# Filler matmuls in planned gaps everywhere, not only in the normalisation zones

## The chip, the core and the metric

The kernel runs on one core of a Trainium2 chip. The metric is device time in microseconds from launch to end, the median of three runs. TensorE (PE) does matmuls and writes PSUM, VectorE (DVE) and ScalarE (ACT) work on PSUM and SBUF, GpSimd (POOL) on SBUF alone, and SyncE (SP) issues the DMAs. TensorE's clock has two levels in the records, 1.2 and 2.4 GHz; a granted clock of 0.50 is the lower one.

## The reference, cut to what matters

Two trunk layers run over 128 context tokens and 512 latent tokens that share every weight, in float32.

```
for l in range(DEPTH):                       # DEPTH = 2, D_MODEL = 1024
    shift1, scale1, gate1, shift2, scale2, gate2 = SiLU(cond) W_mod + b_mod
    u = LN(x) * (1 + scale1) + shift1
    x = LN_1(alpha * x + gate1 * W_out concat_heads[mLSTM | gated DeltaNet | retention | RWKV-7](u W_in))
    u = LN(x) * (1 + scale2) + shift2
    x = LN_2(alpha * x + gate2 * relu(u W_1)^2 W_2)
```

Each mixer has four heads of width 64 and scans forwards and backwards over chunks. DeltaNet and RWKV-7 need, for each 128 tokens, the inverse of a triangular matrix. The fillers of this case compute nothing that the reference asks for: their results are never read.

## The kernel before

**How the work is staged.** A layer has three parts. *Mixing*: weights of `w_in` come in as tiles `wr`, are split into a high part `wh` (ScalarE, sometimes VectorE) and a low part `wl` (GpSimd or VectorE), and are multiplied with the features `uh`, `ul` in three matmuls per block of 128 into PSUM tiles `pj` (`pgj` for the gates). Beside these dense projections run the scans: many small float32 matmuls whose results go through VectorE and ScalarE and back. `solve_blocks` and `inverse` (tiles `ei`, `ew`, `lv`) make the inverses, `step` walks the chunks (`pxx`, `pwx`, `pzz`), and at the end of a mixer stand its outputs (`poo`, `pqs`), its head norm on VectorE (`osum`), its transposes (`pt`), and the result `y`, which goes through DRAM and comes back as `yk`, `yh`, `yl`. *Output and normalisation*: `w_out` (tiles `pwo`), layer norms, transposes to features (`put`). *Feed-forward*: `pj` with features `vh`, `vl`, then `pff`. Modulation (`pmod`, `pmt`, `pmg`, `msb`) for layer 0 begins at once and goes on inside the mixing; that of layer 1 runs beside layer 0's feed-forward part. Of the eight blocks of `y`, the one made last is that of the second DeltaNet pair, and 195 of a layer's 240 `pwo` matmuls come behind its transposes.

**What sets the order.** Nothing is issued as it is written. `Plan.record` notes each operation as a node with an estimated duration. `Plan.schedule` (line 416) then plays the program forward on five engines with those estimates: whenever an engine is free it takes the ready node of highest priority for which PSUM and SBUF have room. `Plan.emit` (line 775 in every profile row) issues the nodes in the order of their planned starts, and each engine keeps strictly to this order. The planner also books how much matmul work TensorE has done lately (`recent - part`, in columns weighted by the cost of the type) and doubles the durations where it thinks the clock is low.

**Fillers.** Where TensorE's queue is empty in the plan, or holds only nodes that may wait a little longer (`early`), the planner may put in a filler: a float32 matmul of 128 x 128 constants (line 810, tile `warm`), which is two passes in the profile. It takes one of eight PSUM banks, must leave two free (`FB`), and isn't used in the first 12 planned microseconds (`FT0`). Before the change it must also be in a zone: a stretch of nodes marked by hand around `w_out`, the layer norms and the transposes to features (`thin()`, and `plan.zones.append` at line 2362). `floor` is the oldest node that has not been planned yet, and is what a zone is compared with. In a zone a filler goes in while the booked work is under 1.3 x 3100 (`FT`).

Of the kernel before, what the change touches and what calls it, by code (L numbers as in the profile page):

```python
# [213 lines left out]
class Plan:  # L214
# [201 lines left out]
    def schedule(self):  # L416
# [34 lines left out]
        caps, load, blocked, order = {}, {}, {}, {}  # L451
# [33 lines left out]
        FT, FT0, FB, FN = 1.3, 12.0, 2, 128  # L485
# [7 lines left out]
        now = 0.0  # L493
        done = 0
        floor = 0
# [3 lines left out]
        early = []  # L499
# [11 lines left out]
        hist, recent = collections.deque(), 0.0  # L511
# [20 lines left out]
        def pe_queue():  # L532
            tops = [(q[0], (128, 128), q) for q in (heaps["PE"],) if q]
            tops += [(q[0], m_, q) for m_, q in tiled.items() if q]
            best = min(tops, key=lambda x: x[0][:2], default=None)
            if dense and (best is None or dense[0][:2] < best[0][:2] or not warm or thin):
                best = (dense[0], (128, 128), dense)
            if best is None:
                while early and early[0][2].end is not None:
                    heapq.heappop(early)  # L540
                return early or None
            if best[1] != mode:
                same = [x for x in tops + ([(dense[0], (128, 128), dense)] if dense else []) if x[1] == mode]
                if same:
                    c = min(same, key=lambda x: x[0][:2])
                    if c[0][0] - best[0][0] < HY:
                        best = c
            return best[2]
# [11 lines left out]
        def filler(now):  # L560
            x = self.warm_tile().tile
            caps[x.key] -= 1
            x.seq = x.at = x.end_seq = floor
            load[x.key][floor] += 1
            x.alloc = True
            nd = Node()
            nd.eng, nd.nm, nd.idx, nd.tiles, nd.preds, nd.succs, nd.grp = "PE", "matmul", len(N) + len(out), [x], [], [], None
            nd.a, nd.k, nd.fn = (x.view()[:, 0:FN],) + self.warm(FN), {}, self.warm_fn
            nd.mem, nd.act, nd.mode = [("matmul", nd.fn, nd.a, nd.k)], self.activity("matmul", nd.a[0], nd.a), self.pe_mode(nd.a)
            nd.dur = self.pe_time(nd.mem)  # L570
            return nd, x

        def eligible(nd, t):
            must = nd.idx == floor
            used, take = {}, []
            for x in nd.tiles:
                if x.alloc:
                    continue
                if not must and x.kind == "psum" and nd.grp is None and not x.open and caps[x.key] - used.get(x.key, 0) <= RES:
                    return x.key, None  # L580
                if not room(x, used):
                    return x.key, None
                used[x.key] = used.get(x.key, 0) + 1
                take.append(x)
            if not must:
                for x in list(take):
                    for p in x.gate.values():
                        if p.end is None or p.end > t + 0.3:
                            return ("g", p), None
                    for p in x.late.values():  # L590
                        if p.end is None:
                            return ("g", p), None
                    for y in x.along:
                        if not y.alloc and y not in take:
                            if not room(y, used):
                                return y.key, None
                            used[y.key] = used.get(y.key, 0) + 1
                            take.append(y)
            return None, take
        gateb = {}  # L600
        wait = {}
        while True:
            progress = True
            while progress:
                progress = False
                for e in engs:
# [3 lines left out]
                    if e == "PE":  # L610
# [3 lines left out]
                        part = 0.0  # L614
                        if hist and hist[0][0] < now + LK - TICK:
                            a_, b_, c_ = hist[0]
                            part = c_ * (now + LK - TICK - a_) / (b_ - a_)
                        thin = recent - part < HM * 3100
                        warm = cols.get(k - 1, 0.0) >= 3100
                    while h or e == "PE" or soon[e]:  # L620
                        q = pe_queue() if e == "PE" else h or soon[e]
                        if e == "PE" and (q is None or q is early) and now > FT0 and recent - part < FT * 3100 and any(a <= floor < b for a, b in self.zones) and caps[self.bank] > FB:
                            nd, x = filler(now)
                            d = nd.dur + (SW if nd.mode != mode else 0.0)
                            mode = nd.mode
                            d *= 1 if warm else 2
                            hist.append((now, now + d, nd.act))
                            recent += nd.act
                            k = int(now / TICK + 1e-9)
                            cols[k] = cols.get(k, 0.0) + nd.act  # L630
                            nd.start = now
                            nd.end = free[e] = now + d
                            out.append(nd)
                            self.nfill += 1
                            heapq.heappush(ev, (free[e], cnt, 1, None)); cnt += 1
                            heapq.heappush(ev, (free[e] + 0.1, cnt, 2, x)); cnt += 1
                            progress = True
                            break
# [19 lines left out]
                        b, take = eligible(nd, now)  # L658
# [81 lines left out]
            now = max(now, ev[0][0])  # L740
# [1775 lines left out]
```

## Time and profile before

| | |
|---|---|
| runs | 2372.74, 2365.53, 2366.48 us |
| median | 2366.48 us |
| profiled execution, its own time | 2367.83 us |
| its span, first to last instruction | 2366.1 us |
| TensorE matmuls busy | 2149.7 us, 91% |
| VectorE / ScalarE / GpSimd busy | 66% / 40% / 33% |
| mean granted clock of TensorE | 0.953 |
| fillers in the program | 188 (376 passes) |

A profile row of the timeline has the start, the time from the start of the first to the end of the last of a merged group, engine, line, operation, output and inputs, shapes and count; in brackets is how long the engine sat idle before and who released it. The parts of the span, by the timeline: start to 56 us, mixing of layer 0 to about 643, output and normalisation to about 764, feed-forward to about 1246, and then the same for layer 1, whose mixing ends at about 1803.

### The profile page before, as it was taken

What the parts mean: (1) busy time and instruction counts of PE and PEld (TensorE: products, weight loads), DVE (VectorE), ACT (ScalarE), POOL (GpSimd) and SP (SyncE); (2) the same over time, 40 slices, a digit from 0 to 9 for tenths busy, and PEclk for the clock granted to TensorE, in tenths of its full rate; (3) what the DMA queues carried; (4) which work ended last, traced back from release to release, by engine and by line L of the source; (5) the groups of instructions that cost most, each with busy time, mean ns of one, the idle gap of its engine ahead of it and who ended that gap; (6) DMA issues with size and microseconds to landing.
All of it is one profiled execution on the core that took longest, in us unless ns stands there. A gap on an engine that the chain in (4) does not pass through costs nothing. (4 is left out here: it accounts for less than half of the span.)

```text
span 2366.1 us, 42824 instructions
## 1 busy us (share of the span) xinstructions
PE 2149.7 (91%) x16886; PEld 1887.9 (80%) x16886; DVE 1557.5 (66%) x3258; ACT 948.1 (40%) x2014; POOL 771.4 (33%) x687
## 2 busy tenths in 40 slices
PE   5998989988887999999979989899888799999997
PEld 2887778777677898889867878798777689999996
DVE  5576768686779657666687768679785843333357
ACT  3434244342335545445344443443441443333332
POOL 2141414433347333334353424324452710000023
PEclk7999989999798999999998989899899999999999
DMA  8132352626443444444541322313353412222242
GB/s 266 28 69 77 102 112 75 172 76 167 147 133 116 140 132 134 134 125 132 173 125 36 74 36 60 88 53 83 102 164 108 151 63 73 80 72 81 71 161 89
DMA packets 317453, 253.17 MB, mean 107 GB/s; under 512 B 91100, under 2 KB 240828, under 8 KB 317252
## 3 DMA queue, kind: packets, MB, share of 16 engines
q1 hardware_dynamic: 317252, 250.43, 37.1%
q8 instruction: 133, 2.18, 0.4%
q14 instruction: 68, 0.56, 0.1%
HBM read 226.14 MB, written 24.24 MB: 106 GB/s over the span
## 5 line engine op out<-in xcount | busy, mean ns | idle before, releaser
L775 ACT CAST wh<-wr 128x1024 fp32r<-128x1024 f32 x233 | 244.3, 1049 | 502.2 <-PE pff L775 214.1
L775 PE MATMUL pff<-wh,hid 128*128 128x512 f32 x1280 | 397.6, 392 | 0.2 <-ACT wh L775 0.2
L775 POOL TENSOR_TENSOR wl<-wr,wh 128x1024 fp32r<-128x1024 f32 x92 | 227.9, 2480 | 407.2 <-ACT wh L775 394.2
L775 DVE TENSOR_TENSOR wl<-wr,wh 128x1024 fp32r<-128x1024 f32 x142 | 186.5, 1313 | 208.8 <-ACT wh L775 208.7
L775 PE MATMUL pj<-uh,wl 128*128 128x256 f32 (+1 forms) x1056 | 312.6, 336 | 8.5 <-POOL wl L775 6.3
L775 PE MATMUL pj<-uh,wh 128*128 128x256 f32 (+1 forms) x1056 | 311.3, 336 | 9.6 <-ACT wh L775 6.3
L775 PE MATMUL pj<-ul,wh 128*128 128x256 f32 (+1 forms) x1056 | 311.9, 334 | 0.0
L775 PE MATMUL pj<-vh,wl 128*128 128x384 f32 (+1 forms) x1024 | 286.7, 312 | 3.5 <-POOL wl L775 3.2
L775 PE MATMUL pj<-vh,wh 128*128 128x384 f32 (+1 forms) x1024 | 284.4, 313 | 5.0 <-ACT wh L775 5.0
L775 PE MATMUL pj<-vl,wh 128*128 128x384 f32 (+1 forms) x1024 | 283.3, 312 | 0.0
L775 PEld LDWEIGHTS pff<-wh,hid 128*128 128x128 f32 x1280 | 238.8, 189 | 51.1 <-ACT wh L775 0.5
L775 PE MATMUL pff<-wl,hid 128*128 128x512 f32 x640 | 245.2, 396 | 9.3 <-POOL wl L775 8.7
L775 PEld LDWEIGHTS pj<-uh,wh 128*128 128x128 f32 x1056 | 194.9, 196 | 27.3 <-issue 10.5
L775 PEld LDWEIGHTS pj<-uh,wl 128*128 128x128 f32 x1056 | 194.9, 196 | 25.9 <-issue 9.9
L775 PEld LDWEIGHTS pj<-ul,wh 128*128 128x128 f32 x1056 | 195.8, 196 | 12.6 <-issue 8.3
L775 PEld LDWEIGHTS pj<-vh,wh 128*128 128x128 f32 x1024 | 186.9, 191 | 9.4 <-ACT wh L775 5.7
L775 PEld LDWEIGHTS pj<-vh,wl 128*128 128x128 f32 x1024 | 185.7, 191 | 6.5 <-POOL wl L775 3.8
L775 PEld LDWEIGHTS pj<-vl,wh 128*128 128x128 f32 x1024 | 185.9, 190 | 2.5 <-issue 1.4
L775 POOL TENSOR_TENSOR mac<-mac,mtm 128x512 f32<-128x512 f32 x77 | 112.4, 1460 | 183.9 <-ACT mtm L775 160.1
L775 DVE TENSOR_TENSOR hid<-sqr,hid 128x384 fp32r<-128x384 f32 (+1 forms) x126 | 77.5, 618 | 129.4 <-ACT hid L775 128.9
L775 DVE SCALAR_TENSOR_TENSOR mac<-wr,cc,mac 128x512 f32<-128x512 f32 x84 | 100.8, 1200 | 78.2 <-DMA wr<-in_w_mod 56.8
L775 POOL TENSOR_TENSOR acc<-acc,bc 128x512 f32<-128x512 f32 x16 | 27.3, 1729 | 382.6 <-DMA xr<-x1d 357.5
(502 smaller groups left out, 4249.5 us busy)
## 6 DMA issues: line engine op xcount, KB each, us to landing
wr<-in_w_ff SPq DMA_DIRECT2D x136, 512.0 KB
wr<-in_w_mod SPq DMA_DIRECT2D x96, 512.0 KB
wr<-in_w_in SPq DMA_DIRECT2D x66, 512.0 KB
wr<-in_w_out SPq DMA_DIRECT2D x32, 512.0 KB
dq<-rscr SPq DMA_DIRECT2D x20, 256.0 KB
dec<-rscr SPq DMA_DIRECT2D x16, 320.0 KB
x1d<-x SPq DMA_DIRECT2D x20, 256.0 KB
xr<-x1d SPq DMA_DIRECT2D x20, 256.0 KB
```

Source lines behind the costliest of these rows:

```text
L775: fn(*[res(v) for v in a], **{k_: res(v) for k_, v in k.items()})
```

## The change

One condition of the planner is widened. Outside the zones a filler may now go in too, if the work booked is under 3100 (without the factor 1.3). All other conditions stay. Nothing else in the kernel is edited.

```diff
--- before.py
+++ after.py
@@ -619,7 +619,7 @@
                     while h or e == "PE" or soon[e]:
                         q = pe_queue() if e == "PE" else h or soon[e]
-                        if e == "PE" and (q is None or q is early) and now > FT0 and recent - part < FT * 3100 and any(a <= floor < b for a, b in self.zones) and caps[self.bank] > FB:
+                        if e == "PE" and (q is None or q is early) and now > FT0 and recent - part < FT * 3100 and (any(a <= floor < b for a, b in self.zones) or recent - part < 3100) and caps[self.bank] > FB:
                             nd, x = filler(now)
```

Since the plan is made forward, a filler changes what is planned behind it, on all engines. The program before has 188 fillers, the program after 225. Numbers behind a name count tiles and differ between the two programs for the same tile.

The first place is TensorE at the start, where the first modulation tiles (`pmod`, with `pmt` and `pmg` behind each) meet the first transposes to features (`put`, whose inputs `xn` are normalised tokens). Before:

```order
L775 MATMUL pmg_253<-cst,msb_216 128x128
L775 MATMUL pmt_270<-msb_263,cst 32x128 x4
L775 MATMUL pmg_288<-cst,msb_263 128x128
L775 MATMUL put_299<-cst,xn_161 128x128
L775 MATMUL put_301<-cst,xn_161 128x128
L775 MATMUL put_303<-cst,xn_161 128x128
L775 MATMUL put_309<-cst,xn_161 128x128
L775 MATMUL put_313<-cst,xn_205 128x128
L775 MATMUL put_319<-cst,xn_205 128x128
L775 MATMUL put_327<-cst,xn_205 128x128
L775 MATMUL put_313<-cst,xn_243 128x128
L775 MATMUL pmod_336<-wr_165,cc 32x512 x2
```

and after:

```order
L775 MATMUL pmg_261<-cst,msb_218 128x128
L810 MATMUL warm_266<-cst 128x128
L810 MATMUL warm_270<-cst 128x128
L775 MATMUL pmt_285<-msb_268,cst 32x128 x4
L810 MATMUL warm_297<-cst 128x128
L810 MATMUL warm_304<-cst 128x128
L775 MATMUL pmg_309<-cst,msb_268 128x128
L810 MATMUL warm_311<-cst 128x128
L775 MATMUL put_314<-cst,xn_161 128x128
L775 MATMUL put_316<-cst,xn_161 128x128
L775 MATMUL pmod_320<-wr_165,cc 32x512 x2
```

Five fillers came in (a sixth stands further up), and six of the eight transposes moved behind the eight `pmod` rows that follow here. A `put` tile of `xn_161` is complete with one transpose; `put_313` needs the two that are seen.

The second place is TensorE in layer 0's mixing, at the `pmt` of a gate's modulation, whose bias comes by DMA; `pj_6547` and `pj_6554` (in the second list `pj_6556` and `pj_6558`) are the two halves of a projection. Before:

```order
L775 MATMUL pj_6291<-uh_478,wl_6262 128x256
L775 MATMUL pmt_6531<-msb_6451,cst 32x128 x4
L775 MATMUL pj_6547<-uh_317,wh_6517 128x384
L775 MATMUL pj_6554<-uh_317,wh_6517 128x256
L775 MATMUL pj_6547<-ul_325,wh_6517 128x384
L775 MATMUL pj_6554<-ul_325,wh_6517 128x256
L775 MATMUL pj_6547<-uh_317,wl_6536 128x384
```

and after:

```order
L775 MATMUL pj_6291<-uh_471,wl_6267 128x256
L810 MATMUL warm_6536<-cst 128x128
L810 MATMUL warm_6542<-cst 128x128
L775 MATMUL pmt_6544<-msb_6452,cst 32x128 x4
L810 MATMUL warm_6549<-cst 128x128
L810 MATMUL warm_6552<-cst 128x128
L775 MATMUL pj_6556<-uh_327,wh_6523 128x384
L775 MATMUL pj_6558<-uh_327,wh_6523 128x256
L775 MATMUL pj_6556<-ul_333,wh_6523 128x384
L775 MATMUL pj_6556<-uh_327,wl_6532 128x384
```

Two fillers stand ahead of `pmt` and two behind it; the first use of `wl` comes one row sooner.

The third place is TensorE at the end of layer 1's mixing, from the last DeltaNet outputs to the transposes `pt` of the normalised `osum`. Before (the last `poo` is the row ahead of the first of 25 `pwo`; the last four of them are shown):

```order
L775 MATMUL pwo_19444<-wh_20007,yl_19400 128x512
L775 MATMUL pwo_19452<-wl_20017,yh_19334 128x512
L775 MATMUL pwo_19448<-wh_20007,yl_19400 128x512
L775 MATMUL pwo_19452<-wh_20007,yl_19400 128x512
L775 MATMUL pt_3315_20073<-cst,osum_19916 128x128
L775 MATMUL pt_3316_20075<-cst,osum_19916 128x128 x4
L810 MATMUL warm_20085<-cst 128x128
```

and after, from the last `poo`:

```order
L775 MATMUL poo_20068<-Rd_19213,dec_18012 128x64
L775 MATMUL poo_20068<-Rd_19213,dec_18105 128x64
L775 MATMUL poo_20068<-Rd_19213,dec_18018 128x64
L775 MATMUL poo_20068<-Rd_19213,dec_18160 128x64
L810 MATMUL warm_20079<-cst 128x128
L810 MATMUL warm_20081<-cst 128x128
```

Sixteen fillers in a row stand there, then `pt` for the first token tile, one filler, `pt` for the other four, and ten fillers. The 25 `pwo` have moved ahead of the last `poo`, among the scan's matmuls. At the end of layer 0's mixing no `pwo` stood between `poo` and `pt` in either program; there ten fillers now stand before the transposes, where none stood, and 13 behind them, where 16 stood.

## Rows read from the trace of the kernel before

**Rows 1.** The page, section 1: busy time of each engine.

```profile
PE 2149.7 (91%) x16886; PEld 1887.9 (80%) x16886; DVE 1557.5 (66%) x3258; ACT 948.1 (40%) x2014; POOL 771.4 (33%) x687
```

**Rows 2.** Groups by line: count, busy, mean ns, idle before and releasers.

```profile
L810 PE MATMUL warm<-cst 128*128 128x128 f32 x376 | 52.0, 296 | 1.5 <-DVE wot L775 1.3 <-ACT relu L775 0.2
```

**Rows 3.** Busy time by stretch: both mixing stages, and places with a low clock.

```profile
core 0: us, PE busy (x) PEld busy (x) DVE busy (x) ACT busy (x) POOL busy (x), PEclk, DMA share, GB/s
50.00:60.00 10.00, 9.20 (x45) 7.67 (x45) 10.00 (x25) 7.21 (x20) 4.93 (x9) 0.65 0.45 137
56.10:643.40 587.30, 535.80 (x5429) 462.90 (x5428) 412.89 (x1125) 225.82 (x581) 194.05 (x190) 0.94 0.39 103
1245.90:1803.10 557.20, 503.75 (x5231) 447.77 (x5230) 418.79 (x1139) 224.20 (x575) 214.17 (x206) 0.94 0.32 79
43.30:56.90 13.60, 10.08 (x48) 7.79 (x48) 12.29 (x26) 9.58 (x23) 4.87 (x5) 0.50 0.73 206
555.30:562.10 6.80, 5.49 (x19) 5.49 (x20) 6.80 (x4) 0.00 (x0) 6.45 (x4) 0.50 0.42 113
633.80:654.20 20.40, 12.29 (x59) 12.13 (x60) 10.99 (x44) 0.00 (x0) 3.45 (x4) 0.50 0.22 76
1818.20:1821.60 3.40, 3.40 (x9) 2.63 (x8) 0.47 (x1) 0.00 (x0) 0.00 (x0) 0.50 0.04 13
```

**Rows 4.** Timeline of TensorE in the first 56 us.

```profile
27.52 1.91 PE L775 MATMUL put<-cst,xn 128*128 128x128 f32 x8
...
40.12 1.06 PE L775 MATMUL pmod<-wr,cc 128*32 128x512 f32 x8 [1.49 <-DMA wr<-in_w_mod]
```

**Rows 5.** Timelines of ScalarE and VectorE: one eviction of a `put` tile.

```profile
30.26 0.56 ACT L775 ACTIVATE u<-put,modT 128x256 f32<-128x256 f32 x1
30.85 0.41 ACT L775 CAST uh<-u 128x256 fp32r<-128x256 f32 x1
...
31.29 0.43 DVE L775 TENSOR_TENSOR ul<-u,uh 128x256 fp32r<-128x256 f32 x1 [0.72 <-ACT uh L775]
```

**Rows 6.** Timeline of TensorE at 362 and at 554 us.

```profile
361.68 0.33 PE L775 MATMUL ptt<-cst,wm 128*128 128x128 f32 x1 [2.70 <-DVE R L775]
...
553.73 0.43 PE L775 MATMUL pmt<-msb,cst 128*32 128x128 f32 x8 [2.69 <-DMA msb<-in_b_mod]
...
556.61 0.90 PE L775 MATMUL pj<-uh,wl 128*128 128x384 f32 x2 [1.67 <-POOL wl L775]
```

**Rows 7.** Timeline of TensorE at the end of layer 0's mixing.

```profile
641.59 1.81 PE L775 MATMUL poo<-Rd,dec 128*128 128x64 f32 x8
651.51 1.30 PE L775 MATMUL pt<-cst,osum 128*128 128x128 f32 x5 [8.12 <-DVE osum L775]
652.60 4.52 PE L810 MATMUL warm<-cst 128*128 128x128 f32 x32
```

**Rows 8.** Timeline of TensorE at the end of layer 1's mixing.

```profile
1802.30 1.00 PE L775 MATMUL poo<-Rd,dec 128*128 128x64 f32 x8
1803.11 0.47 PE L775 MATMUL pwo<-wh,yl 128*128 128x512 f32 x1
...
1810.79 0.74 PE L775 MATMUL pt<-cst,osum 128*128 128x128 f32 x5 [1.68 <-DVE osum L775]
1811.36 3.74 PE L810 MATMUL warm<-cst 128*128 128x128 f32 x32
1817.87 0.53 PE L775 MATMUL pwo<-wh,yh 128*128 128x512 f32 x1 [2.77 <-DVE yh L775]
```

**Rows 9.** Timeline of TensorE: two gaps in layer 1's last solve.

```profile
1769.87 0.21 PE L775 MATMUL lv<-gh,wi 32*32 32x32 f32 x1 [3.77 <-issue]
...
1780.10 0.18 PE L775 MATMUL lv<-gh,ws 32*32 32x32 f32 x1 [4.17 <-issue]
```

**Rows 10.** Timelines of TensorE and VectorE at the end.

```profile
2348.36 7.31 PE L810 MATMUL warm<-cst 128*128 128x128 f32 x64
...
2359.27 2.95 DVE L775 TENSOR_TENSOR xn<-xn,bc 128x512 f32<-128x512 f32 x3
```

## The prediction

> **What bounds the kernel now.** I read the page first. TensorE is busy for 91% of the span [rows 1], no other engine for more than 66%, so time is lost where TensorE waits or runs slowly. Then the stretches [rows 3]: the columns to read are the stretch's length against PE busy, and PEclk. From the first projection to the last `poo` the mixing of layer 0 takes 587.30 us and leaves TensorE idle for 51.50; layer 1 takes 557.20 and leaves 53.45. Both have a granted clock of 0.94, so about 6% x 2 of each is at the lower level (1.2 GHz). Over the whole span the mean clock is 0.953: 0.047 x 2 x 2366.1 = 222 us at 1.2 GHz. Third, the timeline at places where the clock is low.
>
> The only loss that a filler can touch is real matmuls at half rate behind a quiet spell; it does not shorten the wait itself.
>
> **What the change adds, and where.** The lists hold 225 fillers instead of 188. The 37 more are not spread over the mixing stages. By place: six (was two) in the first 56 us; four near 430 us of the old trace, in front of the projection pair that begins there; four around the `pmt` at 553.73; 23 instead of 16 at the end of layer 0's mixing; 27 instead of 16 at the end of layer 1's; 44 instead of 37 behind the last `pff`. Between 1290 us and layer 1's last `poo` there is none. One filler is two passes; 16 in a row take 3.74 us at full clock [rows 8], 0.234 us each, so 37 are 8.7 us of TensorE, if nothing hid them.
>
> Second, the planner works forward, so a filler early on alters what comes after it. Rows of the feed-forward stages and of layer 1's first 100 us stay almost as they were; in both mixing stages about half of the rows trade places with neighbours, though the projections, solves and scans come in the old sequence.
>
> **The sum, place by place.** It is made against the profiled execution, 2367.83 us (span 2366.1 and 1.7 around it), 1.35 above the median of the runs, 2366.48.
>
> *First 56 us.* Before, eight `put` transposes stood ahead of the third modulation tile and ran at 27.52 [rows 4]; five of them completed their tiles and were evicted at once, while ScalarE and VectorE had little else. In the new list two stand there, and the rest behind all eight `pmod` rows, whose last waits for its weights until 40.12 [rows 4]. Three evictions so move into the stretch from 50 to 60 us, where VectorE is busy for 10.00 of 10.00 us [rows 3]. The widest costs 0.56 + 0.41 + 0.43 = 1.40 us of engine time [rows 5]; three, at most 4.2, shared by VectorE and ScalarE: 2.1 us. Lower bound 0, if TensorE's own chain ends later. Since VectorE has no slack there I take +1.5. The fillers themselves lie in waits for `msb` and cost nothing; at 43.30 to 56.90 the clock stays at 0.50 [rows 3], as nothing is added there.
>
> *At 430 us.* The four fillers stand where the old trace shows no wait, so they cost 0 (the reordering made a gap) to 4 x 0.234 = 0.9. I take +0.5.
>
> *At 554 us.* `pmt` waits 2.69 us for the bias's DMA and holds up the projections queued behind it; a little later `pj` waits 1.67 us for `wl` [rows 6]. Behind it 6.80 us run at 0.50, with TensorE busy for 5.49 [rows 3]. Two fillers now stand ahead of `pmt` and two behind. If they keep the clock up, half of 5.49 comes back, -2.7; if not, the two behind, or all four where the DMA is early, cost up to +0.9. The rows speak for both: a quiet spell of 2.70 us at 361.68 [rows 6] did not bring the clock down, so this one is near the edge; but 16 fillers followed by 2.77 us of quiet at 1817.87 [rows 8] did not prevent 3.40 us at 0.50 [rows 3]. I take -1.0, a little under half.
>
> *End of layer 0's mixing.* Ten of the 23 fillers stand between the last `poo` and `pt`, in a wait of 8.11 us (643.40 to 651.51) that VectorE's head norm sets [rows 7]; 2.3 us of fillers (4.7 at half rate) are over well before. If the clock is up by then, the five transposes take 0.74 us as in layer 1 [rows 8] instead of 1.30 [rows 7]: -0.6 to 0, I take -0.3. The 13 behind `pt` replace 16 in a wait for `y`'s way through DRAM and cost nothing.
>
> *End of layer 1's mixing.* Here the order matters more than the fillers. Before, 25 `pwo` stood between the last `poo` and `pt` and filled 6.0 us of a 7.49 us wait, so that TensorE idled only 1.68 [rows 8]. In the new list all 25 stand ahead of the last `poo`, and 16 fillers take their place. If those `pwo` found gaps there, as the 3.77 and 4.17 us before `lv` would be [rows 9], nothing is lost; if not, the last `poo`, and all behind it, comes 6.0 us later. So 0 to +6.0. Those two gaps end inside groups of one solve, which no `pwo` can enter, but the planner placed them into something; I take +2.5, below the middle.
>
> *The end.* The old fillers finish at 2355.67 and VectorE's last work at 2362.22 [rows 10]; seven more, 1.6 us, or 3.3 at half rate, still end under it: 0.
>
> *Reordering in the rest of mixing.* Its sign can't be read from lists. For its size the two layers are a trial that has been made already: the same generators in two rather different orders leave 51.50 and 53.45 us idle, 2 us apart [rows 3]. I take 0, plus or minus 2 per layer.
>
> Sum: 1.5 + 0.5 - 1.0 - 0.3 + 2.5 = +3.2. The profiled execution would be 2371.0, the median 2369.7. Bounds together: -2.7 - 0.6 - 4 = -7.3 and 2.1 + 0.9 + 0.9 + 6.0 + 4 = +13.9. A measurement of this kernel tells about 0.3%, 7.1 us, from no change; +3.2 is within it.
>
> **A rule against this sum.** In the three low stretches that fillers now adjoin (6.80, 20.40 and 3.40 us) TensorE was busy for 5.49, 12.29 and 3.40 [rows 3], so a full clock could give back 2.7 + 6.1 + 1.7 = 10.6 at most. The Trainium skill, "TensorE: Matmul & The Clock Gate", section "Terms", prices time at the lower clock at that time x (1 - K/N), half of it: by the page these stretches would be worth 15.3 us and all 222 us of low clock 111. The trace does not agree for this kernel, because about a third of those three stretches (30.6 us, 21.2 busy) is waiting, which a clock does not shorten.
>
> **The rivals.**
>
> *Fillers hold the clock* at all three stretches: -10.6, 2355.9. For it: they adjoin exactly these. Against it: none is added inside the `poo` and `pqs` run from 633.80, where 6.1 of it lies, and the 16 at 1811.36 did not hold it. Chance 0.14.
>
> *Mixing falls out better* by more than the two layers differ: of 105 us idle some 8 less, 2358.5. The fillers change nothing that aims at this. 0.08.
>
> *Cover used up* (slower): layer 1's 25 `pwo` find no gap, and the three upper bounds apply with it: 6.0 + 2.1 + 0.9 + 0.9 = +9.9, 2376.4. It decides for slower once more than 4 of the 6.0 us are not absorbed and the first 56 us lose their 2. Speaking for it: TensorE has 1.68 us of idle left from 1803 to 1811. Against: the scan's own waits may take the matmuls. 0.27.
>
> *Fillers in the way* (slower): each takes a PSUM bank and a place in TensorE's strict order, and real matmuls behind it wait for the bank's eviction. All 37 on the path are +8.7, 2375.2. Against: the 376 passes of before waited 1.5 us in all [rows 2]. 0.05.
>
> *No change that can be measured*, by the sum above: 0.46. A change that simply does nothing lies in here too.
>
> **How the numbers follow.** Faster by over 0.3%: 0.14 + 0.08 = 0.22. Within: 0.46. Slower: 0.27 + 0.05 = 0.32. The predicted time is the middle case's, 2369.7. The range goes down to the first rival less 2 us for one layer's reordering, 2354, and up to the third, 2376.4, plus 4 for both layers and 2.6 for what I can't name, 2383; about 0.2 is outside.
>
> **What would show it.** A granted clock of 1.00 at the old 555 us place, and `pj` there at full rate, shows that term; 0.50 shows it wrong. The first `pgj`, at 56.10 before, should start 1 to 2 us later. Between layer 1's last `poo` and `pt` TensorE should idle, or run fillers, for some 7 to 8 us. The mixing stages should have idle sums within 2 us of 51.5 and 53.5, with the clock still near 0.94; if one has changed by over 5 us, the reordering was larger than I priced it and the prediction is wrong for that reason. If the low stretch before layer 0's `pt` is gone and with it several microseconds, the first rival was right.

## The result: slower by 1.1%, above the predicted range

| | before | after |
|---|---|---|
| runs | 4 | 4: 2409.55, 2390.30, 2392.11, 2393.46 us |
| median | 2366.86 us | 2392.78 us |
| ratio | | 1.0111, 95% interval 1.0087 to 1.0135 |
| profiled execution, span, clock | 2367.83, 2366.1 us, 0.953 | 2409.55, 2407.8 us, 0.942 |

I had predicted 2369.7 us, 2354 to 2383. The profiled execution of after is the longest of its four, 17 us over the median, so its rows show places and kinds of loss, in sizes that the other three need not have; the whole is taken from medians.

The view by windows of the changed kernel (columns: stretch, its length, busy time and count of PE, PEld, DVE, ACT and POOL, granted clock, DMA share, GB/s): the start, the two mixing stages, the `pmt` of the prediction's 554 us, and the end of layer 1's mixing.

```profile
0.00:56.40 56.40, 30.34 (x153) 11.97 (x153) 27.80 (x79) 18.52 (x38) 12.99 (x24) 0.85 0.87 279
56.40:661.90 605.50, 543.55 (x5448) 470.24 (x5447) 411.99 (x1118) 225.76 (x581) 208.05 (x205) 0.92 0.39 100
1265.40:1843.10 577.70, 519.23 (x5256) 462.25 (x5254) 415.82 (x1134) 224.09 (x573) 209.79 (x214) 0.91 0.32 78
584.00:592.00 8.00, 6.09 (x31) 5.74 (x32) 6.12 (x7) 2.25 (x4) 7.58 (x8) 0.57 0.93 269
1843.10:1851.30 8.20, 3.95 (x36) 3.78 (x35) 5.06 (x26) 0.63 (x1) 2.22 (x2) 0.98 0.02 7
```

Against [rows 3] the mixing stages are longer by 18.2 and 20.5 us, which is 38.7 of the 41.7 by which the spans differ; the other stages kept their lengths. TensorE is idle in them for 605.50 - 543.55 = 61.95 and 577.70 - 519.23 = 58.47 us (before 51.50 and 53.45), and the clock fell from 0.94 to 0.92 and 0.91: about (0.08 x 605.5 + 0.09 x 577.7) x 2 = 201 us at 1.2 GHz instead of 137 (the clock has two decimals, so each of the two is good to some 12 us). So fillers came, and both idle time and low clock rose.

One caution for layer 1: its two windows don't hold the same work. The 25 `pwo` that moved ahead of the last `poo` lie inside the window after and behind it before. TensorE's `pwo` alone, before and after:

```profile
1245.90:1803.10 557.20, 8.97 (x20) 4.57 (x21) 0.00 (x0) 0.94 0.32 79
```
```profile
1265.40:1843.10 577.70, 19.60 (x45) 11.20 (x45) 0.00 (x0) 0.91 0.32 78
```

They take 10.6 us of TensorE there, so up to half of layer 1's 20.5 us may be theirs. Layer 0's windows hold 45 `pwo` each.

The timeline of TensorE after, at the places with the longest new waits and at two that the prediction named (in brackets the idle time before a row, and who ended it):

```profile
204.50 0.27 PE L775 MATMUL lv<-gh,ws 32*32 32x32 f32 x3 [6.51 <-ACT ws L775]
...
585.91 0.65 PE L775 MATMUL pmt<-msb,cst 128*32 128x128 f32 x8 [3.46 <-DMA msb<-in_b_mod]
...
1550.70 0.73 PE L775 MATMUL lv<-gh,wi 32*32 32x32 f32 x37 [7.54 <-issue]
...
1841.67 1.67 PE L775 MATMUL poo<-Rd,dec 128*128 128x64 f32 x14
1843.18 3.79 PE L810 MATMUL warm<-cst 128*128 128x128 f32 x32
1851.23 0.45 PE L775 MATMUL pt<-cst,osum 128*128 128x128 f32 x1 [4.25 <-DVE osum L775]
```

The two waits inside solves, 6.51 and 7.54 us, are longer than at these rows before (3.17 us at 199.10 for the first). Waits of this size are not new as such: a solve of layer 1 waits 7.01 us in before, at 1518.68. No filler stands in either of the two, so the change doesn't reach them.

### The profile page after: what moved, and what is told of

The parts are those of the page before. It is cut to its first block, busy times and chain, and to the rows that moved or that the text cites. A ratio compares the mean times of both kernels' runs of the same rounds, so it can differ in the third digit from the quotient of the medians.

```text
span 2407.8 us, 43009 instructions
## 1 busy us (share of the span) xinstructions
PE 2177.1 (90%) x16960; PEld 1912.9 (79%) x16960; DVE 1551.0 (64%) x3244; ACT 944.4 (39%) x2007; POOL 777.6 (32%) x708
## 4 chain that ended last, share of the span: by engine, by line
PE 51%; DVE 16%; DMA 7%; POOL 5%; issue 4%; ACT 3%; SPq 1%; DVEq 0%; POOLq 0%; ACTq 0%
PE pj L775 24%; PE pff L775 13%; DMA wr<-in_w_mod 3%; PE pwo L775 3%; PE lv L775 2%; DVE xn L775 2%; DVE mac L775 1%; POOL wl L775 1%; PE poo L775 1%; DVE acc L775 1%; DVE lnst L775 1%; SPq L775 1%; DVE lnrs L775 1%; ACT wh L775 1%; DVE osum L775 1%
## 5 line engine op out<-in xcount | busy, mean ns | idle before, releaser
L775 DVE TENSOR_TENSOR wl<-wr,wh 128x1024 fp32r<-128x1024 f32 x151 | 197.6, 1308 | 221.1 <-ACT wh L775 221.1
L775 PE MATMUL pj<-uh,wl 128*128 128x256 f32 (+1 forms) x1056 | 318.0, 338 | 6.6 <-POOL wl L775 4.3
L775 PE MATMUL pj<-uh,wh 128*128 128x384 f32 (+1 forms) x1056 | 315.0, 338 | 6.2 <-DVE dec L775 3.5
L775 PE MATMUL pj<-ul,wh 128*128 128x256 f32 (+1 forms) x1056 | 317.1, 336 | 2.7 <-issue 2.6
L775 POOL TENSOR_TENSOR wl<-wr,wh 128x1024 fp32r<-128x1024 f32 x83 | 205.9, 2484 | 348.3 <-ACT wh L775 320.5
```

The costliest lines, as they stand in the source:

```text
L775: fn(*[res(v) for v in a], **{k_: res(v) for k_, v in k.items()})
```

## Experiments

The first theory was that the new order costs the time: what fillers early in the plan did to the order of the mixing stages (theory A). Its rivals were that the fillers themselves cost it, and that the six at the start are special, since they move the transposes there. Ratios are to the kernel before in the same job; its median was 2368.5 to 2370.2 us in them.

**Order or fillers?** One run keeps after's order on every engine but doesn't issue the 51 fillers that it has outside the zones. The other keeps before's order on every engine, and lays 25 more fillers afterwards into what the plan shows as gaps of TensorE (six at the start, seven at 1666 us, and six more behind each mixing stage's `pt`).

```diff
+ nd.drop = not any(a <= floor < b for a, b in self.zones)
...
+ if getattr(nd, "drop", False):
+     continue
```
```diff
+ while not was and room_ >= FB and t > FT0 and max(nd.start, nd.ready) > t + 0.05:
+     f, x = filler(t)          # laid when the plan is done: no other node moves
```

> The changed kernel's plan with its order on every engine, but none of the 51 fillers that stand outside the zones is issued (174 fillers are left). Theory A (the new order of the mixing stages costs the 26 us): stays slow, about 2390, between 2380 and 2400, with both mixing stages some 18 to 21 us longer than before. Theory B (the added fillers themselves cost: TensorE's time, PSUM banks): back to 2360 to 2374.

Measured 2386.95 (2381.61 to 2391.32), ratio 1.0085 [1.0063, 1.0106], 18.5 us above before. The windows of its mixing stages, in a run of 2391.32 us:

```profile
56.30:649.30 593.00, 533.40 (x5430) 461.27 (x5428) 412.87 (x1118) 226.11 (x582) 208.39 (x205) 0.94 0.39 102
1249.60:1825.30 575.70, 519.58 (x5254) 463.88 (x5252) 414.67 (x1133) 224.03 (x572) 210.24 (x214) 0.91 0.32 79
```

They are 5.7 and 18.5 us longer than before, so the 18 to 21 us expected of both came in layer 1 alone, where the 25 `pwo` take 18.64 - 8.97 = 9.7 us of it by the same view.

> The old plan with its order on every engine, and 25 fillers more laid over its planned TensorE gaps outside the zones (213 in all). Theory A: within 0.3% of before, 2360 to 2374. Theory B: 25 of 37 fillers, so about two thirds of the 26 us, 2380 to 2390. If fillers without a new order hold the clock, 2355 to 2362.

Measured 2371.54 (10 runs, 2365.74 to 2377.90), ratio 1.0010 [0.9996, 1.0025]. The order alone makes most of the loss, and these fillers alone, which stand only in part where after has its own, change nothing that can be told. Between after and its order alone the intervals overlap, so what after's own fillers cost there isn't shown; after is the slower of the two, and no gain shows.

**Which fillers reorder the plan?** Fillers outside the zones only in the first 60 planned us (six of them), and only after that.

```diff
- ... or recent - part < 3100)
+ ... or now < 60 and recent - part < 3100)
```

> Fillers outside the zones only in the first 60 planned us: six at the start, and an order that differs from before in both mixing stages (188 fillers in all). Theory A: the mixing stages move by several us each, the total anywhere from 2360 to 2400, though the fillers end before 35 us. Theory B: six fillers, 2364 to 2372, and mixing stages as long as before.

Measured 2385.29 (2383.20 to 2387.59), ratio 1.0076 [1.0057, 1.0095]. Six fillers that are over by 35 us, with the new order behind them, are enough for a loss of 17 us; in its profile the mixing stages take 598.4 and 564.0 us instead of 587.3 and 557.2. The run with fillers alone had six at the start as well, in the old order, and lost nothing that could be told.

> Fillers outside the zones only after 60 planned us: the order is that of before up to 527 us and then differs, and 47 fillers more are issued, most in layer 1's mixing (235 in all). Theory A: layer 0's mixing is as long as before within 5 us, layer 1's moves by 5 to 25 us either way. Theory B: 47 of 37 fillers' cost, 2395 to 2405, and the time is lost where they stand.

Measured 2356.74 (7 runs, 2349.04 to 2367.88), ratio 0.9961 [0.9937, 0.9985]: faster than before and after. The stages don't do what theory A expected: layer 0's mixing, which should have stayed within 5 us, takes 575.8 us in the profile, and layer 1's 557.8, nearly as before. Its order alone, with the 54 fillers outside the zones not issued:

> The order of the run with fillers only after 60 planned us (2356.7 us), with its 54 fillers outside the zones left out. If its gain of 11 us is its order's (theory A): 2353 to 2361. If it is the fillers', which keep the clock up: 2364 to 2370, with at least 15 us more at 1.2 GHz than with them.

Measured 2373.32, ratio 1.0012 [0.9997, 1.0026]. These two were measured on different chips, so the pair was measured again on one.

> The same kernel as the run with fillers only after 60 planned us, again, beside its own order without those fillers. If their fillers hold the clock: 2352 to 2360 here and 8 us or more under the order alone. If the 17 us between the two runs came of two chips: within 5 us of the order alone.

Measured 2362.92 (12 runs, 2353.84 to 2375.72), ratio 0.9978 [0.9961, 0.9995].

> That order without its 54 fillers outside the zones, again. With fillers that hold the clock: 2365 to 2377. With a difference of chips: 2355 to 2363, as the kernel with them.

Measured 2371.12 (12 runs), ratio 1.0001 [0.9985, 1.0017]. The kernel with fillers came out slower than the first time, but the pair still differs by 8.2 us, half of the 17 that the first pair showed. The two intervals overlap a little; both pairs have the same sign, so in this order fillers do seem to gain. The windows of layer 1's mixing in the two profiles (with fillers, and TensorE's filler passes alone; then the order alone, and the same):

```profile
1237.50:1798.30 560.80, 516.97 (x5302) 461.30 (x5300) 422.80 (x1136) 228.69 (x578) 211.31 (x205) 0.94 0.32 81
...
1237.50:1798.30 560.80, 10.55 (x57) 9.11 (x55) 0.94 0.32 81
```
```profile
1237.60:1807.30 569.70, 515.59 (x5253) 458.66 (x5252) 423.84 (x1136) 228.57 (x579) 211.03 (x205) 0.93 0.32 80
...
1237.60:1807.30 569.70, 1.25 (x9) 0.97 (x7) 0.93 0.32 80
```

Without fillers TensorE's own work takes 515.59 - 1.25 = 514.3 us, with them 516.97 - 10.55 = 506.4: the 7.9 us by which the same matmuls run faster is nearly the whole 8.9 us of the stage.

**Is it these fillers, or any disturbance?** Four runs hold the planner's TensorE once for 0.5 planned us (at 100, 200, 430 or 1300), with nothing issued; a fifth changes a planner constant. No rule for fillers is touched.

```diff
+ if e == "PE" and now > 100.0 and not held:
+     held = True
+     free[e] = now + 0.5
```
```diff
- BLG = 0.4
+ BLG = 0.41
```

> The kernel before, its rules for fillers untouched; once, at 100 planned us, the planner's TensorE is held for 0.5 planned us, and nothing is issued for it. From there on the list differs: 530 of VectorE's 3260 rows move, the start doesn't. Theory A (any small disturbance of the plan deals the mixing stages anew, and that deal is worth 10 to 25 us either way, which is all that the six fillers at the start did): outside 2361 to 2376, most likely slower, 2375 to 2392. Theory B (the fillers at the start are special, since they move six transposes behind the third modulation tile; other disturbances cost what is held, 0.5 us): 2368 plus or minus 5.

Measured 2382.47 (7 runs), ratio 1.0053 [1.0033, 1.0073].

> As the run with the hold at 100 us, but held once at 430 planned us; 486 rows of VectorE move, all behind that place. Theory A: outside 2361 to 2376, either sign, smaller than for the hold at 100 since a part of layer 0's mixing is untouched: 5 to 20 us. Theory B: 2368 plus or minus 5.

Measured 2383.91 (6 runs), ratio 1.0061 [1.0031, 1.0091]. In its profile layer 0's mixing is not slower at all; the loss came in layer 1.

> Held once at 1300 planned us, in layer 1's mixing; 327 rows of VectorE move, layer 0 is as before. Theory A: layer 1's mixing, 557 us before, changes by 4 to 20 us either way, layer 0's by under 3; the total by as much. Theory B: 2368 plus or minus 5, layer 1's mixing within 3 us of 557.

Measured 2366.06 (10 runs), ratio 0.9996 [0.9980, 1.0012]: no change, though 327 rows moved. Theory A failed here for the total. (In its profile, a run of 2373.03 us, layer 1's mixing is 567.5 us long; the 25 `pwo` have moved ahead of the last `poo` here as well.)

> The kernel before with TensorE held in the plan once at 200 planned us for 0.5 us; 333 of 3260 rows of VectorE move. Theory A, now sharper (the order of before is a good deal among many; another deal costs 5 to 25 us and seldom gains): 2373 to 2392. Theory A as first put (either sign alike): as likely 2345 to 2361 as 2376 to 2392. Theory B (only the start matters) is left with 2368 plus or minus 5.

Measured 2396.72 (2394.19 to 2406.20), ratio 1.0119 [1.0095, 1.0143].

> The kernel before with one planner constant at 0.41 instead of 0.40: the weight of the work queued at an operation's first engine when the planner thinks of giving it to the other. 691 of VectorE's 3260 rows move, from about 210 planned us on; no rule for fillers changes. Sharper theory A: 2373 to 2392. Either sign alike: 2345 to 2361 as likely. Small plan changes harmless: 2368 plus or minus 5.

Measured 2402.31 (2395.49 to 2409.61), ratio 1.0136 [1.0115, 1.0157]. Both lie above the 2373 to 2392 of the sharper theory A. A constant changed by a fortieth costs as much as the change under study (33.7 and 25.9 us, with intervals that overlap). Over eight orders other than before's the difference to before is +33.7, +28.1, +18.5, +16.8, +15.0, +13.5, +2.5 (+4.4 in its first job) and -2.9 us. "Either sign alike" fell with this list: six of eight are clearly slower, and none is clearly faster.

**What in the new order costs the time?** At 204.50 the chain behind the wait of 6.51 us is, in the timelines of ScalarE and GpSimd after:

```profile
203.74 0.40 ACT L775 ACTIVATE dq<-dq,ga 128x128 f32<-128x128 f32 x1 [7.50 <-POOL dq L775]
204.04 0.41 ACT L775 COPY ws<-lv 128x320 f32<-128x320 f32 x1
...
202.44 1.26 POOL L775 TENSOR_TENSOR dq<-dq,cst 128x512 f32<-128x512 f32 x1 [9.73 <-DMA dq<-rscr]
```

`ws`, which the solve waits for, stands on ScalarE behind `dq`, whose data are late. I exchanged the two rows, and the like pair at 1549 us (`dq` ahead of `vtok`); nothing else moves.

```diff
+ if (name(x), name(y)) in (("dq_444", "ws_337"), ("dq_2800", "vtok_2685")):
+     i, j = out.index(x), out.index(y)
+     out.insert(j, out.pop(i))
```

> The changed kernel with two neighbouring pairs of rows on ScalarE exchanged and nothing else: in each, an activation of dq, whose data come late by DMA and GpSimd, no longer stands ahead of a copy that the solve waits for (ws at 204 us, vtok at 1549 us; TensorE waits 6.51 and 7.54 us there). If the new deal is slow by such inversions in the strict order of one engine, each exchange gives back 4 to 7 us of the wait and some of the low clock behind it: 2392.8 less 8 to 20, 2373 to 2385. If what comes next is late too (dq is needed anyway), the wait is only passed on: 2388 to 2396.

Measured 2403.59 (6 runs, 2390.79 to 2415.32), ratio 1.0143 [1.0111, 1.0176]: no gain, and above both ranges. ScalarE's and TensorE's timelines of that run:

```profile
196.43 0.43 ACT L782 COPY ws<-lv 128x320 f32<-128x320 f32 x1 [0.53 <-PE lv L782]
...
207.27 0.27 PE L782 MATMUL lv<-gh,ws 32*32 32x32 f32 x3 [8.18 <-issue]
...
1542.01 0.79 PE L782 MATMUL lv<-gh,wi 32*32 32x32 f32 x42 [8.74 <-issue]
```

`ws` is there 7.6 us sooner, and TensorE still waits as long, now for nothing that the profile names. So the inversion was real but only passed the wait on. In the order-alone run, too, the first of these solves waits only 3.55 us, at 205.37, and the kernel is slow all the same. The transfers are the next thing to read. SyncE's issues after, ahead of that solve, and the DMA view of 192 to 200 us:

```profile
189.71 0.36 SPq L775 DMA_DIRECT2D out_mC<-zs  x1
190.12 0.43 SPq L775 DMA_DIRECT2D out_mn<-zs  x1
190.66 0.38 SPq L775 DMA_DIRECT2D dq<-rscr  x1
```
```profile
DMA packets 71, 0.07 MB, mean 9 GB/s; under 512 B 0, under 2 KB 71, under 8 KB 71
...
q1 hardware_dynamic: 71, 0.07, 95.0%
```

The times of the packets that start there fill 95% of 16 engines' 8 us, and these packets move 9 GB/s. The packets of 1024 bytes, `dq` among them, take up to 8.4 us; the median of this size is 0.046. In every profile up to here stand packets of 5 to 9 us, one or two groups of them, within some 5 us behind an `out_mn` store: 128 values written as 4-byte elements. Before has them at 327 to 337 us, behind the `out_mn` issued at 325.79, and again at 1399 to 1407. Only two of before's eight stores are followed by packets that long; behind three more, packets take 2.3 to 3.3 us. So I left these eight stores out of either order.

```diff
+ if nd.eng == "SP" and isinstance(nd.k["in_"], View) and nd.k["in_"].tile.kw["name"].startswith("zs") and nd.k["in_"].shape[-1] == 1:
+     continue
```

> The kernel before, every engine's order untouched, but its eight stores out_mn (128 values of 4 bytes each) are left out, so this output isn't written. In the traces so far, once or twice per layer DMA packets that follow such a store take 7 to 10 us each, TensorE's instruction loads among them; before has this at 327 to 337 and 1399 to 1407 us, both inside solves. If the store causes it: no packets over 5 us in mixing, solve at 311 us shorter by 8 to 14, in all 8 to 20 us faster, 2349 to 2361. If it is something else that only follows it in time: 2364 to 2373.

Measured 2334.31 (2331.70 to 2346.22), ratio 0.9856 [0.9832, 0.9879]: 35 us, well beyond what I had worked out. No packet takes over 1.9 us any more. The two long stalls alone, some 10 us each, don't add up to 35; how the rest divides over the shorter ones and the clock isn't shown. The solve at 311 us, first in the kernel before, then without the stores:

```profile
311.00:347.70 36.70, 31.08 (x603) 25.33 (x602) 16.11 (x40) 17.61 (x50) 4.89 (x3) 0.81 0.47 80
```
```profile
306.80:333.50 26.70, 25.27 (x601) 20.87 (x602) 15.56 (x40) 17.89 (x50) 4.89 (x3) 1.00 0.38 113
```

Ten us shorter for the same rows, of which TensorE's busy time is 5.8, at a clock of 1.00 instead of 0.81.

> The changed kernel without its eight out_mn stores, which here stand just ahead of the solves at 183 and 1412 us. If the new deal is slow because it moves these stores to where they hurt more: 22 to 35 us faster than with them, 2358 to 2371, close to the kernel before without them. If the store costs both orders about the same: 2372 to 2384, still 15 us or more behind. If the store costs nothing: 2388 to 2400.

Measured 2361.49 (12 runs, 2352.02 to 2366.29), ratio 0.9962 [0.9944, 0.9979]. The changed order gains 31 us as well and stays 27.2 us behind before's order without them, where it was 25.9 behind with them. The time lies in the first of the expected ranges, but that one's condition, close to before without the stores, isn't met: both orders lose about the same. The stall is a large loss of both kernels, and not what tells them apart.

**Fillers where the waits really are.** Before's order untouched, with 178 more fillers ahead of rows of TensorE that waited over 1.5 us in its trace. The list has 24 rows and 198 fillers; by the trace three of the rows got none, since fillers are laid only where the plan has a PSUM bank free.

```diff
+ AIM = {228: 7, 651: 8, 936: 9, 1227: 10, 1855: 5, 1885: 5, 1979: 8,
...
+ for i in range(AIM.get(r, 0) if room_ >= 1 else 0):
+     f, x = filler(nd.start)
+     f.start = f.end = nd.start - 1e-6 * (AIM[r] - i)
```

> The order of before, untouched on every engine, with 178 more fillers put ahead of 24 rows of TensorE in the two mixing stages that waited over 1.5 us in the trace of before (4 to 22 fillers each, by the length of the wait), instead of in gaps of the plan. If fillers hold the clock where the waits really are: less time at 1.2 GHz in mixing, 137 us before, by 40 us or more, and 8 to 25 us faster, 2343 to 2361. If they don't hold it, or hold up real matmuls for as much: 2362 to 2376. If they run over their waits at half rate, slower, 2376 to 2390.

Measured 2365.56 (12 runs, 2354.44 to 2373.26), ratio 0.9983 [0.9962, 1.0004]: the interval takes in no change. The windows of its mixing stages, all of TensorE and the filler passes alone:

```profile
55.70:644.10 588.40, 543.87 (x5573) 469.76 (x5572) 414.02 (x1126) 226.89 (x583) 195.13 (x191) 0.96 0.39 102
1242.40:1798.90 556.50, 516.25 (x5435) 464.09 (x5433) 418.65 (x1137) 223.08 (x573) 212.15 (x205) 0.98 0.32 80
...
55.70:644.10 588.40, 19.86 (x146) 18.42 (x145) 0.96 0.39 102
1242.40:1798.90 556.50, 30.67 (x213) 28.45 (x211) 0.98 0.32 80
```

and the filler passes of before in its own windows:

```profile
56.10:643.40 587.30, 0.34 (x2) 0.05 (x1) 0.94 0.39 103
1245.90:1803.10 557.20, 1.23 (x9) 0.95 (x7) 0.94 0.32 79
```

The clock did rise, from 0.94 to 0.96 and 0.98, and the same matmuls take 543.87 - 19.86 + 516.25 - 30.67 = 1009.6 us instead of 535.80 - 0.34 + 503.75 - 1.23 = 1038.0 [rows 3], 28 us less. But the stages are as long as before: 588.40 + 556.50 = 1144.9 against 1144.5. The 28 us went into waiting (idle or filled). I read this so: in these places other engines or transfers set the pace, and a faster TensorE only arrives sooner.

**A version that beats both.** All outputs, with `out_mn` turned into rows of 32 values by one VectorE transpose before each store; on before's order, and on that with fillers only after 60 us.

```diff
+ nc.vector.transpose(out=t, in_=col.to_broadcast([128, 32]))
+ nc.sync.dma_start(out=out.rearrange("(b k) o -> b (k o)", b=4), in_=t[0:128:32, :])
```

> The kernel before with all its outputs, TensorE, ScalarE and GpSimd in their old order; out_mn is turned into rows by one VectorE transpose each (8 in all, 128x32), and stored as 4 runs of 128 bytes instead of 128 of 4. If the 4-byte elements made the stall: as without these stores, 2331 to 2343, no DMA packets over 5 us. If any store at that place makes it: 2360 to 2372.

Measured 2339.60 (2337.01 to 2341.68), ratio 0.9880 [0.9859, 0.9900]. The form of the store, 128 pieces of 4 bytes, made the stall, and not a store at that place: the store stayed, and the longest packet takes 2.0 us. Whether the size of the pieces or their number does it isn't separated, since both changed.

> The same for the order with fillers only after 60 planned us (6 to 12 us under before). If its gain is its fillers' and not a matter of where the stall fell: 2320 to 2335, 4 us or more under the other run of this pair. If it was only a luckier place of the stall: within 4 us of it or above.

Measured 2331.83 (2329.16 to 2334.77), ratio 0.9846 [0.9821, 0.9871]: 7.8 us under the other, with ranges apart. It is the fastest version here, 38 us under before. Its order differs from the other's, so this pair shows that the gain doesn't hang on the stall, and not that it is the fillers' alone.

## Why the prediction was wrong

**The step that failed** is "Reordering in the rest of mixing", "plus or minus 2 per layer". Its size was argued from two layers whose idle sums are 2 us apart, called "a trial that has been made already". The runs show +18.5 us for after's order alone, and -3 to +34 us for the eight orders together. Per layer the order alone is 5.7 and 18.5 us longer in its profile; even if all of the 9.7 us of moved `pwo` are put to the term for the end of layer 1's mixing, 5.7 and 8.8 us are left, both beyond 2. In the profile of after, the longest of its runs, it is 18.2 and 20.5. Two things were wrong in the argument. Two layers of one plan say little about the next plan; a few runs of disturbed plans would have given the size (a single one might have shown the -3 us). And idle sums leave out TensorE's own time: beside 10.5 + 5.0 = 15.5 us of new idle time TensorE is busy for 7.75 + 15.48 = 23.2 us more in the two stages. Of these 3.6 are fillers and 10.6 the moved `pwo`; the other 9 are the same matmuls running longer, with some 64 us more at 1.2 GHz. The test written into the prediction, an idle sum changed by over 5 us, is met in both stages, in layer 1 barely (5.02). Why this order is the slower one stays open.

**The other terms.** The start, +1.5: the first projection begins at 56.40 instead of 56.10, so +0.3, within its bounds. The four fillers at 430 us, +0.5: not told apart from the rest. The `pmt`, -1.0: the clock there is 0.57 and its wait 3.46 us instead of 2.69, so the gain didn't come. The end of layer 0's mixing, -0.3: the five `pt` at 669.08 still take 1.30 us at a clock of 0.50, so it wasn't up by then; from the last `poo` to them it takes 7.3 us instead of 8.1. The end of layer 1's mixing: from the last `poo` to `pt` it takes the 7 to 8 us that I named, 1843.18 to 1851.23; the term's cost is the 25 `pwo`, which I bounded by the 6.0 us that they took behind `poo`. Inside the mixing they take 10.6 us, so the bound was too low; how much of it the kernel pays can't be told. They alone don't make an order slow: five of the eight orders move them so, with +33.7, +18.5, +13.5, +2.5 and -2.9 us, and the three that leave 19 to 26 `pwo` behind `poo` are at +28.1, +16.8 and +15.0. The end: the last `pff` stands 17.5 us ahead of the span's end, 18.0 before, so 0 as said. Apart from the `pwo`, none of these terms is off by more than a few microseconds.

**The rivals.** "Cover used up" has the right sign and 10 of the 26 us, by the wrong mechanism. "Fillers hold the clock" is half true. Aimed at real waits they hold it, for 28 us of matmul time, but 3.7 us of the whole, not told from 0; in the one order where they showed a gain it is 8. By the rule that the prediction cites, the Trainium skill, "TensorE: Matmul & The Clock Gate", section "Terms", half of the time at the lower clock is the loss. The aimed run has (1 - 0.953) x 2366.1 x 2 = 222 less (1 - 0.968) x 2360.6 x 2 = 151 us there, 71 less, which by the rule is 36 us. The matmul time of the mixing stages comes near it (28 us), the kernel's time does not (3.7, not told from 0).

**What stays open.** Why the orders differ, by up to 34 us as they are, and by 27 between after and before with the stall gone. In after the loss is spread over the mixing stages as more idle time and more low clock, and exchanging two pairs of rows didn't bring it back. Why before's order is among the best of nine isn't shown either. And why fillers gain 8 us in one order and nothing in two others.

## What to carry to other kernels

Where a planner or scheduler sets the order, a change that feeds back into the plan must be tested in two parts: the new order without the new instructions, and the new instructions in the old order. Give a reordering the spread that a few meaningless disturbances of the plan show (here -3 to +34 us), and not a small number around zero. Look for long packets in the DMA records before aiming at waits on the engines, since here one store of 4-byte elements held up what followed it.

## What the runs showed of the hardware

- **Behind a store of 128 elements of 4 bytes, DMA packets took up to 9.2 us.** Eight such stores, 4 KB of output in all, cost before 35 us and after 31, though in before only two of them are followed by packets of over 5 us. As 128-byte runs they cost nothing that could be told from 0 (2339.6 with the stores, 2334.3 without, medians of two jobs).
- **TensorE's own instructions seem to come by DMA and can be late.** The DMA view has packets of 16384 bytes on a queue that it calls instruction, 133 of them in before. That they are TensorE's is inferred: its 33772 matmul and weight-load rows [rows 1] make 254 for each. I set the waits of over 1 us that the profile gives to "issue" against these packets. In the profiles of the last two versions and of before without the stores, all 20 such waits end 1.2 to 1.6 us after such a packet's end, a stretch that makes up some 2% of the time. Elsewhere most do: 7 of 9 in before, 6 of 8 in after, 5 of 7 with the two pairs exchanged, 2 of 3 in after without the stores. The wait at 1542.01 above, 8.74 us, ends 1.42 us after one; that of 8.18 us at 207.27 doesn't follow one so. 17 of the 20 stand in the solves (`lv`), where up to 80 small matmuls come in a burst. Beside a stall such a packet took 8.8 us in the run held at 200 us, and 1.04 by the median of before. The Trainium skill, "Runtime: NRT & Kernel Launch", section "Instruction fetch mechanics", says that an engine loads its instructions in blocks of 16 KiB over a DMA queue of its own, and calls the cost of crossing into the next block "mostly hidden". The size agrees; here waits of 1 to 9 us end right behind such a load, so there it is not hidden.
